# Strassen pairs of an output projection: one running weight sum instead of two, another product order, and other queues for the row stores

## The chip, the cores and the metric

One core of one Trainium2 chip runs the whole program. The metric is the device time of one execution in microseconds (us). Five engines work side by side and meet at semaphores: TensorE (PE), VectorE (DVE), ScalarE (ACT), GpSimd (POOL) and SyncE (SP, which here only issues transfers). ScalarE and GpSimd can issue transfers too.

## What is computed

Two encoder layers on 512 positions by 2048 features, in float32, then a last RMS norm. Each layer ends in a projection `mixed @ w_out` of 2048 by 2048 that is added to `x`; the next layer begins with the RMS norm of the result.

```python
def hybrid_layer(x, ...):
    h = rms_norm(x, norm_w)
    proj = jnp.einsum('bsd,de->bse', h, w_in)
    ...   # attention, short convolution and gated unit, each normed and gated
    mixed = jnp.concatenate([o_attn, o_conv, o_sgu], axis=-1)
    return x + jnp.einsum('bse,ed->bsd', mixed, w_out)

for layer in range(DEPTH):          # DEPTH = 2
    x = hybrid_layer(x, ...)
return rms_norm(x, final_norm_w)
```

## The kernel before, in words

Every float32 operand of a matmul is split into a high part (`wH`, a cast by ScalarE, line 98) and a remainder (`wL`, a subtraction by VectorE, line 99); three matmuls (high by high, low by high, high by low) make one product. `weight_parts` keeps five buffers of each part, so that the splits can run five weight tiles ahead of TensorE.

The input projection runs as 12 `product` calls per layer (line 201): eight weight pairs of 512 KB each, loaded by SP with `load_pair`, into four PSUM accumulators.

The output projection is the place of the change. `pair` (line 588) computes two column blocks `b0` and `b1` of 512 columns at a time by a scheme of Strassen and Winograd: rows are halved into two halves of 256 positions, the inner dimension into two halves of 1024, and seven products numbered 1 to 7 take the place of eight. One product is 8 inner tiles by 2 row tiles by 3 matmuls of 512 columns: 48 matmuls; a pair has 336, a layer two pairs, (0, 1) and (2, 3). The left operands (`A11`, `A12`, `A22` and the mixed sums `N1` to `N4`) are made by VectorE in `lower`, `mixed` and `upper`. The right operands are sums of four quarters of the weights, held in four tiles `X[i]` and four tiles `Y[i]` of 512 KB. In the order 1, 7, 3, 6, 5, 2, 4:

- `X` is loaded with the first quarter (line 591) and serves product 1. `Y` is loaded with the second quarter (line 593), and GpSimd issues an accumulating transfer that adds the third to it (line 594); it serves product 7. When product 1 has split `X[i]`, GpSimd issues an accumulating transfer of `Y[i]` onto `X[i]` (line 630), for product 6.
- Product 3 loads the third quarter afresh, and VectorE subtracts it from `X[i]` into `Y[i]` (line 632), for product 5.
- After product 6 has split `X[i]`, the fourth quarter is added by an accumulating transfer (line 634), for product 4. Product 2 loads the fourth quarter afresh.

Results go from PSUM to tiles `C[b, st]`: `begin` (line 576) copies by ScalarE and lets GpSimd issue an accumulating transfer of `x`; `gather` (line 582) adds further products by VectorE. A tile with all its products goes through `complete`. In layer 0 (line 710) that is: sum of squares by ScalarE, a store of the tile to DRAM issued by GpSimd (`x1d`, line 713), a transpose in blocks by VectorE (`Rows.put`, line 696), and after every second tile a store of 512 KB to `mv` issued by GpSimd (line 700). `arrive(b)` (line 718) loads `mv` back by SP (line 707) and scales it by ScalarE (line 725); that is the input of layer 1. In layer 1 (line 767) GpSimd multiplies some tiles with the last norm's weights (line 765), and `leave` scales and stores the rest.

Who works when: each engine takes its instructions in one fixed order, written when the kernel is built. Here the framework chooses that order by its own simulation of the program, so an engine's order is not that of the source; SP, ScalarE and GpSimd each hold their transfers in the same order as their other instructions. GpSimd is the only engine that issues accumulating transfers here.

Of the kernel before, what the change touches and what calls it, by code (L numbers as in the profile page):

```python
# [33 lines left out]
def trunk_kernel(ctx: ExitStack, tc: tile.TileContext, xT, xn, win, wout, wcols, convw, qkw, sgun,  # L34
# [224 lines left out]
    for l in range(L):  # L259
# [261 lines left out]
        def mixed(k, i):  # L521
            c, o = lo_of[k], hi_of[k]
            t, u = T(), T()
            nc.vector.tensor_tensor(out=u[:, :HALF], in0=c[:, :HALF], in1=c[:, HALF:], op=ALU.subtract)
            nc.vector.tensor_tensor(out=t[:, :HALF], in0=c[:, HALF:], in1=o[:, HALF:], op=ALU.subtract)
            nc.vector.tensor_tensor(out=t[:, HALF:], in0=t[:, :HALF], in1=c[:, :HALF], op=ALU.subtract)
            nc.vector.tensor_tensor(out=u[:, HALF:], in0=o[:, :HALF], in1=t[:, HALF:], op=ALU.add)
            for (a, b), src, g in (((N3, N4), u, free[2 * i]), ((N1, N2), t, free[2 * i + 1])):
# [40 lines left out]
        wy = [big.tile([P, 2, 2, S], F32, tag="kv", name=nm("wy"), bufs=2) for _ in range(2)]  # L569
        X = [wx[i // 2][:, i % 2] for i in range(4)]  # L570
        Y = [wy[i // 2][:, i % 2] for i in range(4)]
# [16 lines left out]
        def pair(b0, b1, C, complete, held, then={}):  # L588
            s0, s1 = wout[l, b0], wout[l, b1]
            for i in range(4):  # L590
                nc.sync.dma_start(out=X[i], in_=s0[i])
            for i in range(4):
                nc.sync.dma_start(out=Y[i], in_=s1[i])
                nc.gpsimd.dma_start(out=Y[i], in_=s1[4 + i], accum_op=ALU.add)
            c1 = [psum("sc") for _ in range(2)]
            c7 = [psum("acc") for _ in range(2)]
            for p in (1, 7, 3, 6, 5, 2, 4):
                if p == 1 or p == 6:
                    bank = c1
                elif p == 7 or p == 4:  # L600
                    bank = c7
                else:
                    bank = [psum("sc" if p == 2 else "acc") for _ in range(2)]
                A = operand[p]

                def matmuls(t, k, H, Lo):
                    ts = slice(t * P, (t + 1) * P)
                    a, c = A[k][0][:, ts], A[k][1][:, ts]
                    nc.tensor.matmul(bank[t], a, H, start=(k == 0 and p not in (6, 4)), stop=False, skip_group_check=True)  # L609
# [4 lines left out]
                for i in range(4):  # L614
# [4 lines left out]
                    else:  # L619
                        w = Y[i] if p in (7, 5) else X[i]  # L620
                    if held and p == 4:
                        for j in range(2):
                            H, Lo = [res.tile([P, S], F32R, tag=f"x{free[2 * (2 * i + j) + 1]}", name=nm("v"), bufs=2)
# [4 lines left out]
                    parts_i = [weight_parts(w[:, j]) for j in range(2)]  # L628
                    if p == 7:
                        nc.gpsimd.dma_start(out=X[i], in_=Y[i], accum_op=ALU.add)  # L630
                    elif p == 3:
                        nc.vector.tensor_tensor(out=Y[i], in0=X[i], in1=w, op=ALU.subtract)
                    elif p == 6:
                        nc.gpsimd.dma_start(out=X[i], in_=s0[4 + i], accum_op=ALU.add)
                    for j in range(2):
                        for t in range(2):
                            matmuls(t, 2 * i + j, *parts_i[j])
                for t in range(2):
# [6 lines left out]
                    elif p == 3:  # L645
                        begin(C, b1, t, bank[t], 1.0)
                    elif p == 6:
                        begin(C, b0, 2 + t, bank[t], 1.0)
                        gather(C, b1, t, bank[t], ALU.subtract)
                        gather(C, b1, 2 + t, bank[t], ALU.subtract)  # L650
                    elif p == 5:
                        gather(C, b1, t, bank[t], ALU.add)
                        gather(C, b1, 2 + t, bank[t], ALU.add)
                        if t == 1:
                            for st in range(ST):
                                complete(b1, st, bank[st % 2])
# [181 lines left out]
```

## Time and profile before

| what | value |
|---|---|
| median of 3 runs | 1497.47 us (1497.13 to 1497.98) |
| the profiled execution | 1496.9 us |
| its span, first to last instruction | 1494.9 us |
| TensorE busy | 1464.4 us, 98% |
| VectorE, ScalarE, GpSimd busy | 956.2, 680.8, 151.7 us |
| mean granted TensorE clock | 0.991 |
| moved by transfers | 241.64 MB |

The profiled execution stands 0.6 us under the median, and 2.0 us of it lie around the span. Busy shares are averages over a program with stages of different limits; a matmul counts as busy from its start to its modelled end, and consecutive ones overlap, so a stretch in which TensorE starts a matmul every 227 ns is as full as it gets.

### The profile page before, as it was taken

How to read it: one execution, taken by the hardware profiler on the slowest of the kernel's cores; microseconds unless marked ns; L12 is line 12 of the kernel's file. 1: busy time of each engine (PE TensorE's matmuls, PEld its weight loads, DVE VectorE, ACT ScalarE, POOL GpSimd, SP SyncE). 2: the span in 40 equal slices, each digit the busy share in tenths (PEclk: the TensorE clock that was granted, in tenths of full speed). 3: DMA queues.
4: the chain of work that ended last, by engine and by line, in shares of the span. 5: the costliest groups of instructions: out<-in, count | busy, mean ns of one | idle time of the engine just before them, and what ended most of it. 6: DMA issues, size and time to landing. Idle time of an engine off the chain costs nothing.

```text
span 1494.9 us, 18417 instructions
## 1 busy us (share of the span) xinstructions
PE 1464.4 (98%) x6422; PEld 1207.4 (81%) x6422; DVE 956.2 (64%) x1832; ACT 680.8 (46%) x1253; POOL 151.7 (10%) x166
## 2 busy tenths in 40 slices
PE   9999999999999999988989999999999999999997
PEld 7888888888888888866878888888888888888885
DVE  7657898645543467756746578986455534677666
ACT  7333365533332446536643343555333334465554
POOL 0110000000111001222200100000000110012232
PEclk9999999999999999999999999999999999999998
DMA  7334677633236634899863445776233376348975
GB/s 279 102 110 141 188 213 222 183 92 94 90 111 199 209 101 95 203 269 232 208 183 127 113 141 172 220 222 189 85 99 92 100 210 198 100 100 190 260 160 162
DMA packets 77117, 241.64 MB, mean 162 GB/s; under 512 B 9440, under 2 KB 10720, under 8 KB 74208
## 3 DMA queue, kind: packets, MB, share of 16 engines
q1 hardware_dynamic: 62784, 198.49, 42.6%
q0 software_dynamic: 13952, 41.95, 13.8%
q8 instruction: 50, 0.82, 0.2%
q14 instruction: 43, 0.35, 0.1%
q10 hardware_dynamic: 288, 0.03, 0.0%
HBM read 195.35 MB, written 36.70 MB: 155 GB/s over the span
## 4 chain that ended last, share of the span: by engine, by line
PE 91%; DMA 4%; issue 2%; POOL 1%; ACT 1%; DVE 1%; SPq 0%; POOLq 0%; ACTq 0%; DVEq 0%
PE acc L216 61%; PE sc L216 9%; PE acc L609 3%; PE acc L611 3%; PE acc L610 3%; PE sc L609 2%; PE sc L610 2%; PE sc L611 2%; PE sc L355 1%; PE ps L379 1%; PE sc L353 1%; PE ps L381 1%; PE sc L354 1%; PE ps L380 1%; DMA wx<-in_wout 1%
## 5 line engine op out<-in xcount | busy, mean ns | idle before, releaser
L99 DVE TENSOR_TENSOR wL<-wr,wH 128x512 fp32r<-128x512 f32 x448 | 304.1, 686 | 352.9 <-ACT wH L98 324.8
L98 ACT CAST wH<-wr 128x512 fp32r<-128x512 f32 x448 | 275.8, 621 | 522.6 <-PE acc L216 384.9
L216 PE MATMUL acc<-x,wH 128*128 128x512 f32 x1408 | 436.6, 389 | 0.0
L216 PE MATMUL acc<-wH,x 128*128 128x512 f32 x1280 | 393.1, 391 | 5.0 <-ACT wH L98 5.0
L216 PEld LDWEIGHTS acc<-x,wH 128*128 128x128 f32 x1408 | 264.2, 188 | 55.0
L216 PEld LDWEIGHTS acc<-wH,x 128*128 128x128 f32 x1280 | 240.5, 188 | 56.8 <-ACT wH L98 6.8
L216 PE MATMUL acc<-x,wL 128*128 128x512 f32 x704 | 273.2, 389 | 0.0
L216 PE MATMUL acc<-wL,x 128*128 128x512 f32 x640 | 244.6, 390 | 0.0
L216 PEld LDWEIGHTS acc<-x,wL 128*128 128x128 f32 x704 | 132.1, 188 | 27.4
L216 PEld LDWEIGHTS acc<-wL,x 128*128 128x128 f32 x640 | 120.3, 188 | 25.5 <-DVE wL L99 0.4
L99 DVE TENSOR_TENSOR wL<-wx,wH 128x512 fp32r<-128x512 f32 x88 | 60.2, 709 | 44.5 <-ACT wH L98 30.0
L105 POOL TENSOR_TENSOR s<-s,negh 128x4 f32<-128x4 f32 (+2 forms) x44 | 52.2, 1189 | 348.9 <-DVE s L103 343.5
L216 PE MATMUL sc<-wH,x 128*128 128x512 f32 x256 | 78.8, 389 | 0.0
L98 ACT CAST wH<-wx 128x512 fp32r<-128x512 f32 x88 | 52.7, 618 | 49.8 <-DMA wx<-in_wout 12.4
L609 PE MATMUL acc<-wH,n 128*128 128x512 f32 x192 | 74.7, 389 | 0.0
L610 PE MATMUL acc<-wH,n 128*128 128x512 f32 x192 | 74.7, 389 | 0.0
L362 ACT ACTIVATE p<-sc,sa 128x512 f32<-128x512 f32 x64 | 44.1, 689 | 61.4 <-DVE sa L359 43.3
L611 PE MATMUL acc<-wL,n 128*128 128x512 f32 x192 | 66.4, 391 | 1.1 <-DVE wL L99 0.9
L116 POOL TENSOR_TENSOR rc<-s,negh 128x4 f32<-128x4 f32 x5 | 5.1, 1013 | 514.3 <-DVE s L115 514.3
L216 PEld LDWEIGHTS sc<-wH,x 128*128 128x128 f32 x256 | 48.0, 188 | 10.0
L99 DVE TENSOR_TENSOR wL<-wy,wH 128x512 fp32r<-128x512 f32 x64 | 44.6, 720 | 9.7 <-ACT wH L98 6.7
L216 PE MATMUL sc<-wL,x 128*128 128x512 f32 x128 | 49.8, 389 | 0.0
(234 smaller groups left out, 2022.6 us busy)
## 6 DMA issues: line engine op xcount, KB each, us to landing
wr<-in_win SPq DMA_DIRECT2D x191, 512.0 KB, 3.6
rearr<-mv SPq DMA_DIRECT2D x104, 256.0 KB, 5.2
mv<-blk SPq DMA_DIRECT2D x22, 1024.0 KB, 4.8
wr<-in_wout SPq DMA_DIRECT2D x32, 512.0 KB, 4.8
wy<-in_wout SPq DMA_DIRECT2D x16, 512.0 KB, 6.8
wy<-in_wout POOLq DMA_DIRECT2D x16, 512.0 KB, 10.1
wx<-in_wout SPq DMA_DIRECT2D x16, 512.0 KB, 9.4
wx<-wy POOLq DMA_DIRECT2D x16, 512.0 KB, 5.2
```

Of the source, the lines that this page charges most:

```text
L98: nc.scalar.copy(H, src)
L99: nc.vector.tensor_tensor(out=Lo, in0=src, in1=f32(H), op=ALU.subtract)
L105: nc.gpsimd.tensor_tensor(out=r, in0=v, in1=negh[:, :n], op=ALU.pow)
L216: nc.tensor.matmul(acc[e], a, b, start=(kp == kps[0] and j == 0 and i == 0), stop=(kp == kps[-1] and j == 1 and i == 2))
L353: nc.tensor.matmul(sc, qH[:, ss], kH, start=True, stop=False)
L354: nc.tensor.matmul(sc, qH[:, ss], kL, start=False, stop=False)
L355: nc.tensor.matmul(sc, qL[:, ss], kH, start=False, stop=True)
L362: nc.scalar.activation(p, sc, AF.Exp, scale=SCALE, bias=nm_, accum_out=su)
L379: nc.tensor.matmul(po, a, pH[:, t], start=(t == 0), stop=False)
L609: nc.tensor.matmul(bank[t], a, H, start=(k == 0 and p not in (6, 4)), stop=False, skip_group_check=True)
L610: nc.tensor.matmul(bank[t], c, H, start=False, stop=False, skip_group_check=True)
L611: nc.tensor.matmul(bank[t], a, Lo, start=False, stop=(k == 7), skip_group_check=True)
```

## The change

In words: `Y` serves product 7 only and is taken from the pool anew in each pair. `X` grows three times by accumulating transfers straight from DRAM: the second quarter after product 1, the third after product 5, the fourth after product 6. The subtraction of line 632 and the transfer from `Y` to `X` are gone. The order is 1, 7, 5, 2, 6, 3, 4. Products 5 and 3 share two PSUM banks, and two of the twelve `gather` of a pair fall away. The operands in `mixed` are paired anew, `upper` is called after product 5. In layer 0 the `x1d` stores are issued by SP instead of GpSimd and the `mv` stores by ScalarE instead of GpSimd; `arrive` is called after products 5 and 2 of the second pair and, for blocks 3 and 2, inside the first product of layer 1, whose inner order changes. In layer 1 the last norm's weights are loaded after product 7, and GpSimd multiplies ten tiles instead of six.

```diff
-    def product(src, feature_major, before=None, kps=range(KT // 2)):
+    def product(src, feature_major, before=None, kps=range(KT // 2), then={}):
...
-        for kp in kps:
+        for n, kp in enumerate(kps):
+            if n in then:
+                then[n]()
...
-            acc = product(win[l, 0], False, kps=kps)
+            acc = product(win[l, 0], False, kps=kps, then=late)
...
-            for (a, b), src, g in (((N3, N4), u, free[2 * i]), ((N1, N2), t, free[2 * i + 1])):
+            for (a, b), src, g in (((N3, N1), t, free[2 * i]), ((N2, N4), u, free[2 * i + 1])):
...
+            wy = [big.tile([P, 2, 2, S], F32, tag="kv", name=nm("wy"), bufs=2) for _ in range(2)]
+            Y = [wy[i // 2][:, i % 2] for i in range(4)]
...
-            for p in (1, 7, 3, 6, 5, 2, 4):
...
+            c5 = [psum("acc") for _ in range(2)]
+            banks_of = {1: c1, 6: c1, 7: c7, 4: c7, 5: c5, 3: c5}
+            grow = {1: s1[:4], 5: s1[4:], 6: s0[4:]}
+            for p in (1, 7, 5, 2, 6, 3, 4):
+                bank = banks_of[p] if p in banks_of else [psum("sc"), psum("ps")]
...
-                        w = Y[i] if p in (7, 5) else X[i]
+                        w = Y[i] if p == 7 else X[i]
...
-                    parts_i = [weight_parts(w[:, j]) for j in range(2)]
-                    if p == 7:
-                        nc.gpsimd.dma_start(out=X[i], in_=Y[i], accum_op=ALU.add)
-                    elif p == 3:
-                        nc.vector.tensor_tensor(out=Y[i], in0=X[i], in1=w, op=ALU.subtract)
-                    elif p == 6:
-                        nc.gpsimd.dma_start(out=X[i], in_=s0[4 + i], accum_op=ALU.add)
+                    now = [weight_parts(w[:, j]) for j in range(2)]
+                    if p in grow:
+                        nc.gpsimd.dma_start(out=X[i], in_=grow[p][i], accum_op=ALU.add)
...
                     elif p == 5:
-                        gather(C, b1, t, bank[t], ALU.add)
                         gather(C, b1, 2 + t, bank[t], ALU.add)
...
+                    elif p == 6:
+                        begin(C, b0, 2 + t, bank[t], 1.0)
+                        begin(C, b1, t, bank[t], -1.0)
+                        gather(C, b1, 2 + t, bank[t], ALU.subtract)
+                        complete(b1, 2 + t, bank[t])
+                    elif p == 3:
+                        gather(C, b1, t, bank[t], ALU.add)
+                        complete(b1, t, bank[t])
...
-                        nc.gpsimd.dma_start(out=self.m[:, :, st - 1:st + 1],
+                        nc.scalar.dma_start(out=self.m[:, :, st - 1:st + 1],
...
-                nc.gpsimd.dma_start(out=x1d[b, st], in_=c)
+                nc.sync.dma_start(out=x1d[b, st], in_=c)
...
-            pair(2, 3, C, complete, False, {6: lambda: arrive(1), 5: lambda: arrive(0), 2: lambda: arrive(3)})
+            pair(2, 3, C, complete, False, {5: lambda: arrive(0), 2: lambda: arrive(1)})
...
-            arrive(2)
-            kps = (2, 3, 0, 1, 6, 7, 4, 5)
+            kps, late = (0, 1, 2, 3, 6, 7, 4, 5), {4: lambda: arrive(3), 6: lambda: arrive(2)}
...
+            for b in range(2):
+                for st in (0, 2, 1, 3):
+                    weighted(b, st)
...
-        pair(2, 3, C, complete, True, {3: weights_of_the_last_norm})
+        pair(2, 3, C, complete, True, {7: weights_of_the_last_norm})
```

## Rows read from the trace of the kernel before

**Rows 1.** Chain that ended last: start us, us, what; a steady stretch of layer 0.
```profile
52.66 87.07 PE acc L216 x384
```
**Rows 2.** Timeline of TensorE: start us, us, instruction, [idle before it <-releaser].
```profile
580.51 0.39 PE L609 MATMUL sc<-wH,a 128*128 128x512 f32 x1
...
645.14 0.50 PE L609 MATMUL acc<-wH,hA 128*128 128x512 f32 x1 [2.19 <-ACT wH L98]
...
663.50 1.21 PE L611 MATMUL acc<-wL,hA 128*128 128x512 f32 x2 [4.20 <-DVE wL L99]
...
678.48 0.79 PE L609 MATMUL sc<-wH,a 128*128 128x512 f32 x1 [5.84 <-ACT wH L98]
...
751.70 0.39 PE L611 MATMUL acc<-wL,hA 128*128 128x512 f32 x1
...
758.57 1.63 PE L216 MATMUL acc<-wH,x 128*128 128x512 f32 x4 [3.76 <-ACT wH L98]
...
1329.56 0.39 PE L609 MATMUL sc<-wH,a 128*128 128x512 f32 x1
...
1483.70 0.39 PE L611 MATMUL acc<-v,hA 128*128 128x512 f32 x1
```
**Rows 3.** Windows: stretch, its us, busy per engine, granted clock, DMA share, GB/s.
```profile
580.50:667.00 86.50, 80.11 (x337) 65.15 (x336) 64.14 (x105) 48.04 (x91) 22.04 (x28) 0.96 0.82 208
667.00:752.00 85.00, 79.16 (x338) 64.84 (x337) 55.82 (x86) 50.25 (x94) 20.60 (x28) 0.96 0.88 225
1329.50:1405.00 75.50, 75.50 (x333) 62.02 (x333) 57.57 (x94) 45.50 (x88) 15.77 (x18) 1.00 0.84 204
1405.00:1484.00 79.00, 77.94 (x342) 63.63 (x340) 58.70 (x85) 42.24 (x81) 26.25 (x24) 1.00 0.69 162
752.00:830.00 78.00, 74.24 (x321) 60.71 (x320) 40.42 (x91) 32.86 (x63) 5.96 (x8) 0.98 0.50 154
...
580.50:600.00 19.50, 19.50 (x87) 16.14 (x86) 19.50 (x36) 16.16 (x31) 3.52 (x4) 1.00 0.60 108
...
660.00:680.00 20.00, 10.66 (x36) 8.34 (x37) 8.77 (x14) 3.21 (x7) 5.46 (x8) 0.84 0.86 243
```
**Rows 4.** Timeline of GpSimd, its transfers: start us, us, issue, [idle before <-releaser].
```profile
461.08 1.06 POOL L594 DMA_DIRECT2D wy<-in_wout  x1 [1.33 <-PE sc L216]
...
470.60 0.91 POOL L594 DMA_DIRECT2D wy<-in_wout  x1 [4.72 <-issue]
...
631.28 0.89 POOL L594 DMA_DIRECT2D wy<-in_wout  x1 [8.03 <-DVE wL L99]
...
657.73 0.74 POOL L700 DMA_DIRECT2D mv<-blk  x1 [4.59 <-issue]
```
**Rows 5.** Transfers, window 461.0 to 461.25: issue, KB each, us to landing.
```profile
wy<-in_wout POOLq DMA_DIRECT2D x1, 512.0 KB, 9.3
```
**Rows 6.** Chain that ended last, around the waits: start us, us, what.
```profile
666.67 11.04 DMA wx<-in_wout
...
739.81 7.04 DMA mv<-blk
```
**Rows 7.** Timelines of VectorE and of SP's queue around 663 us.
```profile
661.57 1.30 DVE L696 STREAM_TRANSPOSE blk<-p 128x512 f32<-128x512 f32 x2 [8.13 <-DMA mv<-blk]
...
665.27 1.29 SPq L707 DMA_DIRECT2D rearr<-mv  x3
```
**Rows 8.** Queues in window 1328 to 1334, one accumulating transfer: packets, MB, share.
```profile
q0 software_dynamic: 144, 0.52, 46.2%
```
**Rows 9.** Queues, window 562.9 to 566.5: one plain load of 512 KB.
```profile
q1 hardware_dynamic: 144, 0.52, 47.8%
```
**Rows 10.** Lines 632, 152, 765: duration ns min/median/max, first and last start us.
```profile
L632 DVE TENSOR_TENSOR wy<-wx,wr x16: 1215/1222/1226, 594.4 to 1428.5; 128x1024 f32<-128x1024 f32 x16
L152 SPq DMA_DIRECT2D mv<-blk x24: 326/327/338, 70.6 to 1248.3; - x24
L765 POOL TENSOR_TENSOR c<-c,fr x5: 1279/1742/3067, 1443.1 to 1473.1; 128x512 f32<-128x512 f32 x5
```

More of the change, by code (lines that the diff above doesn't have):

```diff
@@ L523, in mixed @@
             t, u = T(), T()
[L524 to L527, printed above, removed]
-            for (a, b), src, g in (((N3, N4), u, free[2 * i]), ((N1, N2), t, free[2 * i + 1])):
+            nc.vector.tensor_tensor(out=t[:, :HALF], in0=c[:, :HALF], in1=c[:, HALF:], op=ALU.subtract)
+            nc.vector.tensor_tensor(out=t[:, HALF:], in0=c[:, HALF:], in1=o[:, HALF:], op=ALU.subtract)
+            nc.vector.tensor_tensor(out=u[:, :HALF], in0=t[:, HALF:], in1=c[:, :HALF], op=ALU.subtract)
+            nc.vector.tensor_tensor(out=u[:, HALF:], in0=o[:, :HALF], in1=u[:, :HALF], op=ALU.add)
+            for (a, b), src, g in (((N3, N1), t, free[2 * i]), ((N2, N4), u, free[2 * i + 1])):
                 h, lo = [res.tile([P, S], F32R, tag=f"x{g}", name=nm("n"), bufs=2) for _ in range(2)]
@@ L608, in matmuls @@
                     a, c = A[k][0][:, ts], A[k][1][:, ts]
-                    nc.tensor.matmul(bank[t], a, H, start=(k == 0 and p not in (6, 4)), stop=False, skip_group_check=True)
+                    nc.tensor.matmul(bank[t], a, H, start=(k == 0 and p not in (6, 3, 4)), stop=False,
+                                     skip_group_check=True)
                     nc.tensor.matmul(bank[t], c, H, start=False, stop=False, skip_group_check=True)
@@ L619, in pair @@
                     else:
-                        w = Y[i] if p in (7, 5) else X[i]
+                        w = Y[i] if p == 7 else X[i]
                     if held and p == 4:
                         for j in range(2):
-                            H, Lo = [res.tile([P, S], F32R, tag=f"x{free[2 * (2 * i + j) + 1]}", name=nm("v"), bufs=2)
+                            H, Lo = [res.tile([P, S], F32R, tag=f"x{free[2 * (2 * i + j)]}", name=nm("v"), bufs=2)
                                      for _ in range(2)]
@@ L627, in pair @@
                         continue
[L628 to L634 removed]
+                    now = [weight_parts(w[:, j]) for j in range(2)]
+                    if p in grow:
+                        nc.gpsimd.dma_start(out=X[i], in_=grow[p][i], accum_op=ALU.add)
                     for j in range(2):
                         for t in range(2):
[L637 removed]
+                            matmuls(t, 2 * i + j, *now[j])
                 for t in range(2):
@@ L749, in leave @@
                 o = C[b, st]
-                if st < 2 or b == 2:
+                if b == 2 or b == 3 and st < 2:
                     nc.vector.scalar_tensor_tensor(out=o, in0=o, scalar=r, in1=fr[b], op0=ALU.mult, op1=ALU.mult)
@@ L758, in weights_of_the_last_norm @@
         def weights_of_the_last_norm():
+            f = big.tile([P, 4, S], F32, tag="kv", name=nm("fr"), bufs=2)
             for b in range(4):
-                f = res.tile([P, S], F32, tag=f"x{free[2 * b]}", name=nm("fr"), bufs=2)
-                nc.sync.dma_start(out=f, in_=frow[b * S:(b + 1) * S].partition_broadcast(P))
-                fr.append(f)
+                nc.sync.dma_start(out=f[:, b], in_=frow[b * S:(b + 1) * S].partition_broadcast(P))
+                fr.append(f[:, b])
+            for b in range(2):
+                for st in (0, 2, 1, 3):
+                    weighted(b, st)
         def weighted(b, st):
@@ L768, in complete @@
             squares(b, st, junk)
-            if b == 3 and st == 3:
-                for bb, ss in ((0, 2), (1, 2), (3, 2), (0, 3), (1, 3), (3, 3)):
-                    weighted(bb, ss)
-            if b == 2:
+            if b == 3 and st > 1:
+                weighted(b, st)
+            if b == 2 and st > 1 or b == 3 and st < 2:
                 leave(st)
         C = tiles(0, 1, False)
-        pair(0, 1, C, complete, False, {7: upper})
+        pair(0, 1, C, complete, False, {5: upper})
         cs_ = [big.tile([P, 2, S], F32, tag="o", name=nm("c"), bufs=2) for _ in range(2)]
```

21 lines of the change are left out of this document (2 added, 19 removed).

## The prediction

> **What bounds the kernel now.** I read the engines first: TensorE is busy 98% of the span, so at most some tens of us can be won, and they must lie where TensorE waits. To find them I compare each stage with a steady stretch: 384 matmuls in 87.07 us, 0.2267 us each [rows 1]. The two pairs of layer 0 have 2 x 336 = 672 matmuls, 152.4 us at that pace. They run from 580.51 to 751.93 (the last start and one pace more), 171.4 us [rows 2]: 19.0 us are lost. The same 672 in layer 1 run from 1329.56 to 1483.93, 154.4 us: 2.0 lost. From 752 to 830, across the change of layers, 321 matmuls take 72.8 of 78 us [rows 3]: 5.2 lost. Together 26.2 us. Nothing else that the change touches delays TensorE, and the tail of 11 us after the last matmul keeps its form.
>
> The waits are four: 2.19, 4.20, 5.84 and 3.76 us [rows 2]. After each, TensorE also runs slowly for a while: the granted clock was 0.84 from 660 to 680, after two waits, and 0.96 over each pair of layer 0 against 1.00 in layer 1 [rows 3]; the level between 1.2 and 2.4 GHz falls after the idling, and that is why 19.0 exceeds the three waits of layer 0 (12.2) by 6.8.
>
> Then I ask why layer 0 and layer 1, with the same products in the same order, differ by 17 us. Layer 0 alone has the stores `x1d` and `mv`, both in GpSimd's order. GpSimd's issues show a limit: the fourth transfer onto `Y` went out at 470.60, after 4.72 us of idling that nothing visible ends [rows 4], and the first, issued at 461.08, had landed 9.3 us later, at 470.4 [rows 5]. So here GpSimd had three accumulating transfers of 512 KB on the way and no more. An `mv` store stands the same way: 4.59 us before the one at 657.73 [rows 4]. Its lateness is what TensorE feels. VectorE waited 8.13 us for an `mv` store to leave its buffer, with `wL` splits behind the transpose [rows 7]: the wait at 663.50. SP held loads for `arrive` ahead of two `X` loads, and a load issued at 666.67 took 11.04 us [rows 6, 7]: the wait at 678.48. At the change of layers an `mv` store of 7.04 us [rows 6] and its loads stand ahead of weight casts on ScalarE: the wait at 758.57. The wait at 645.14 is of another kind: GpSimd idled 8.03 us up to the prefetch of the next `Y` at 631.28 [rows 4], because `Y` is in use until product 5, and a `begin` stood behind it.
>
> **The change part by part.** *Queues.* Per pair of layer 0 GpSimd loses 8 `x1d` and 4 `mv` and gains 4 growths: 32 transfers become 24. ScalarE's own issue of `mv` has no row; the nearest is SP's, 0.327 us [rows 10], so 8 x 0.33 = 2.6 us on an engine busy 98.3 of 171.5 us [rows 3]: hidden, unless ScalarE waits at it for the transposes. That wait blocks the casts behind it, and VectorE's `wL` and TensorE after them; five split buffers, 5 x 6 matmuls = 6.8 us, cover it. Bounds: 0 to 10 us, I take 0. SP's `x1d` waits for the tile, with weight loads behind it; the same cover, the same price.
>
> *Y.* It is free after product 7, so its next load and accumulation can be done three products earlier. The wait at 645.14 goes.
>
> *X.* Each growth has two products, 21.8 us, from split to next use. Issue and landing took 9 to 12 us where transfers crowd [rows 5, 6], so about 8 us of lateness is absorbed. The order of growths and `begin` on GpSimd adds lateness, up to a few us.
>
> *VectorE.* It loses 8 subtractions of 1.22 us and 4 gathers per layer. It was busy 64 of 86.5 us [rows 3] and on no path except behind the transposes: worth nothing beyond what is counted.
>
> *Traffic.* This is the cost. Per pair 12 accumulating transfers of 512 KB become 16. Alone, one occupied the 16 transfer engines for 46.2% of 6 us, 2.77 us [rows 8]; a plain load 47.8% of 3.6 us, 1.72 us [rows 9]. So each layer gains 8 x 2.77 = 22.2 us of transfer work. Busy now: in layer 0 0.82 x 86.5 + 0.88 x 85 = 145.7 us, in layer 1 0.84 x 75.5 + 0.69 x 79 = 117.9 us [rows 3]. The new sums: 168 and 140 us. Layer 0's exceeds the 152.4 us of its matmuls. Not all is waited for: by the start of the last product (141.5 us) six `x1d` (0.86 each, half a plain load), two `mv`, four `arrive` loads and four weight loads of the next layer, 5.2 + 3.4 + 3.4 + 6.9 = 19 us, need not have landed, and block 3's four loads, 3 us, move out. So 146 us are due in 141.5, and the engines idle at first, for lack of work (share 0.60 in the first 19.5 us [rows 3]), some 10 us. Lateness: 146 + 10 - 141.5 = 15 us, of which 8 are absorbed: 7 us of waiting stay in layer 0. In layer 1: 140 less 7 for eight stores of the output, plus 10, is 143 against 141.5: absorbed.
>
> *Layer change.* `arrive(3)` and `arrive(2)` now stand inside the first product, whose first four weight pairs need only blocks 0 and 1, ready earlier. Of 5.2 us I leave 1.2 (bounds 0 and 5.2).
>
> *Layer 1's norm weights.* GpSimd does ten multiplications of 1.3 to 3.1 us [rows 10] instead of six, eight of them while it also issues growths: 8 x 1.7 = 14 us inside two products' time. Against that, 2.0 us of waits may go. I take no change (bounds: 2 won, 8 lost).
>
> *Weighed against a rule.* The trace has GpSimd idle at its issue until an earlier transfer landed [rows 4, 5]; by it the move is worth the waits at 663.50, 678.48 and 758.57. The Trainium skill, page "DMA: Bandwidth & Descriptors", section "Issuing engines are not separate DMA queues", says that transfers from all issuing engines run on the same 16 engines and that spreading them saves only sequencer time. By that rule 8 x 0.7 us of issue would be saved and all waits kept. The rows speak against it for `mv`, and for it in that the sum of traffic stays.
>
> **Sum.** Lost now 26.2; left 7 + 1.2 + 2 = 10.2; won 16.0. The profiled execution took 1496.9 us (2.0 of them around its span); 1496.9 - 16.0 = 1480.9, and the median of the runs stands 0.6 above it: 1481.5.
>
> **Rivals.**
> A, the forecast: 1481.5, own range 1475 to 1488. Chance 0.50.
> B, clean: transfers absorb each other and all waits of layer 0 and the layer change go, 24.2 us: 1473, down to 1470. For it: the first pair of layer 1 runs at a share of 0.84 without a wait [rows 3]. Against: the 168 us. Chance 0.15.
> C, the queue was not the cause: the 16 engines are, and each transfer lands as late as now. Of 26.2 nothing is won, small shifts either way: 1494.5 to 1500. For it: landings of 8 to 11 us in crowded stretches [rows 5, 6], whoever issues. The rule above gives this. Against: 657.73. Chance 0.13.
> D, slower: growths become the bound. It decides when less than 22.2 us of a layer's idle transfer time is usable. Idle are 171.5 - 145.7 = 25.8 us in layer 0 and 154.5 - 117.9 = 36.6 in layer 1. If half is usable, 22.2 - 12.9 = 9.3 and 22.2 - 18.3 = 3.9 us come on top and no wait is won: 1497.5 + 13.2 = 1510.7. For it: the idle time lies at the stages' ends, where nothing is ready. Against: stores need not be awaited. Chance 0.12.
> E, the change doesn't free what it frees on paper: the built order puts ScalarE or SP at a store before its data, with weight loads or casts behind. Price: 8 such stands of up to 3 us, half covered: 10 us of the 16 go back, 1491. Chance 0.10.
>
> **How the numbers follow.** A is likeliest: 1481.5. About 0.2%, 3 us, is what a measurement of this kernel can tell from no change. Faster: A, B, E, 0.75; same: most of C, 0.13; slower: D, 0.12. The range from 1470 to 1497 takes in B, A, E and half of C; outside lie D and the rest, below 2 in 10.
>
> **What would show it.** Right: no idle before GpSimd's issues longer than 3 us that only a landing ends; granted clock near 1.00 in both pairs of layer 0; transfer share above 0.9 there; pairs of layer 0 in about 160 us. Wrong by D: waits of TensorE on casts of `wx`, with growths landing after 12 us and more, in both layers. Wrong by C: the same waits at the same products. Wrong by E: idle ScalarE or SP before line 700 or 713.

## The result and the profile after

The changed kernel takes 1520.36 us (median of 4 runs, 1518.6 to 1521.26), the kernel before beside it 1497.3: a ratio of 1.0152, 95% interval 1.0134 to 1.0169. The forecast was 1481.5 and the range ended at 1497: the sign was wrong, and the time is that of no rival. D, the slower one, came nearest in kind and stood at 1510.7.

The profiled execution has a span of 1518.0 us against 1494.9. The page's engine and transfer totals after the change:

```profile
PE 1470.6 (97%) x6422; PEld 1211.0 (80%) x6422; DVE 936.2 (62%) x1806; ACT 681.3 (45%) x1255; POOL 155.6 (10%) x162
...
DMA packets 83517, 250.03 MB, mean 165 GB/s; under 512 B 9696, under 2 KB 15072, under 8 KB 80608
```

VectorE is relieved by 20 us and 8.4 MB more are moved, both as the diff says. TensorE's waits, from its timeline (start, duration, instruction, [idle before it <-releaser]), answer [rows 2]:

```profile
581.22 0.39 PE L609 MATMUL sc<-wH,a 128*128 128x512 f32 x1
...
624.23 0.79 PE L612 MATMUL sc<-wL,hA 128*128 128x512 f32 x1 [4.31 <-DVE wL L99]
...
665.21 1.22 PE L612 MATMUL acc<-wL,hA 128*128 128x512 f32 x2 [5.28 <-DVE wL L99]
...
697.62 0.80 PE L609 MATMUL acc<-wH,n 128*128 128x512 f32 x1 [6.22 <-ACT wH L98]
...
769.15 2.07 PE L218 MATMUL acc<-wH,x 128*128 128x512 f32 x4 [3.80 <-ACT wH L98]
...
1338.78 0.39 PE L609 MATMUL sc<-wH,a 128*128 128x512 f32 x1
...
1380.73 0.79 PE L612 MATMUL sc<-wL,hA 128*128 128x512 f32 x1 [3.26 <-DVE wL L99]
...
1464.95 0.50 PE L612 MATMUL sc<-wL,hA 128*128 128x512 f32 x1 [4.63 <-DVE wL L99]
...
1505.76 0.39 PE L612 MATMUL acc<-v,hA 128*128 128x512 f32 x1
```

Counted as in the prediction (672 matmuls of two pairs need 152.4 us), the two pairs of layer 0 now run from 581.22 to 759.75: 178.5 us, 26.1 lost where 19.0 were. Those of layer 1 run from 1338.78 to 1505.99: 167.2 us, 14.8 lost where 2.0 were. So 19.9 of the 23.1 us lie in the pairs; 1.4 came between the layers' pairs, 0.7 before them, 1.1 at the end. (Two shorter waits of layer 0, 1.15 us at 744.12 and 1.56 at 755.04, are not shown above.)

The windows answer [rows 3]; the columns are stretch, its us, busy time of PE, PEld, DVE, ACT, POOL, granted clock, DMA share, GB/s:

```profile
581.20:672.20 91.00, 81.41 (x338) 66.28 (x336) 58.30 (x99) 47.55 (x92) 20.03 (x23) 0.92 0.95 238
672.20:759.80 87.60, 78.68 (x338) 64.00 (x337) 51.30 (x82) 49.98 (x96) 16.55 (x19) 0.96 0.93 224
1338.80:1421.40 82.60, 79.34 (x337) 65.08 (x336) 55.17 (x93) 48.45 (x92) 20.09 (x23) 0.96 0.93 224
1421.40:1506.00 84.60, 78.99 (x337) 63.61 (x335) 51.82 (x73) 41.28 (x78) 33.85 (x31) 0.98 0.72 153
...
620.00:640.00 20.00, 15.77 (x59) 12.86 (x60) 12.18 (x20) 7.13 (x15) 5.51 (x7) 0.83 1.04 228
660.00:680.00 20.00, 14.79 (x55) 12.02 (x56) 12.85 (x21) 9.70 (x19) 3.48 (x4) 0.83 0.96 280
```

Share times stretch gives transfer work of 86.5 + 81.5 = 168 us in layer 0 and 76.8 + 60.9 = 138 us in layer 1. The prediction worked out 168 and 140. The sums were right; what they do to TensorE was not.

Four of the waits, 17.5 us together, end at `wL` on VectorE, and VectorE itself now waits long for `x` (who, line, released by: us in total, times, longest):

```profile
DVE c L584 <- DMA c<-x: 23.7, 7, 7.8
...
DVE c L584 <- DMA c<-in_xn: 17.3, 4, 8.0
```

In the kernel before, gathers waited for `x` 5.8 us in all. L584 is `gather`: VectorE adds a product's bank to an accumulator whose `x` is still on its way. The chain into the wait at 624 shows the order (start, duration, what):

```profile
600.04 6.37 DMA wy<-in_wout
...
610.49 0.86 POOL wy L596
...
612.96 0.86 POOL c L580
...
615.55 7.24 DMA c<-in_xn
...
622.88 0.06 DVE c L584
...
623.49 0.69 DVE wL L99
...
624.23 0.79 PE sc L612
```

Product 7 ended at about 603 (the pair's start and 96 paces); its `x` went out only behind the accumulations onto the next pair's `Y`, landed at 622.8, and the `wL` splits stood behind the gather on VectorE. The waits at 665.21, 1380.73 and 1464.95 stand behind such gathers in the same way. After each such wait the granted clock falls (0.83 in the two windows), and a matmul takes 0.43 us instead of 0.23, the lower of the two levels, 1.2 instead of 2.4 GHz: 11.1 us more after these four waits. Waits and slow matmuls make 28.6 us; against that the kernel before's waits at 645.14 and 663.50 are gone (663.50 stood behind an `mv` store [rows 7], the new one at 665.21 behind `x`).

The longest wait, at 697.62, is of another kind. ScalarE, whose casts TensorE wants, stands at the scaling in `arrive` (line 720 here) until the loads of `mv` have landed:

```profile
694.50 2.56 ACT L720 ACTIVATE t<-rearr,wc 128x512 f32<-128x512 f32 x4 [9.47 <-DMA rearr<-mv]
```

Layer 1 shows the waits on `x` best, since no store goes out in it before 1502. GpSimd's timeline in its first pair:

```profile
1351.88 1.79 POOL L580 DMA_DIRECT2D p<-x  x2 [4.69 <-ACT p L578]
1358.04 0.86 POOL L596 DMA_DIRECT2D wy<-in_wout  x1 [4.37 <-DVE wL L99]
1360.30 0.86 POOL L596 DMA_DIRECT2D wy<-in_wout  x1 [1.40 <-DMA wy<-in_wout]
1360.90 1.17 POOL L631 DMA_DIRECT2D wx<-in_wout  x1
1366.92 0.88 POOL L596 DMA_DIRECT2D wy<-in_wout  x1 [4.85 <-issue]
1369.41 0.86 POOL L580 DMA_DIRECT2D c<-x  x1 [1.61 <-ACT wH L98]
1371.93 0.86 POOL L580 DMA_DIRECT2D c<-x  x1 [1.67 <-issue]
```

and VectorE's:

```profile
1377.79 0.69 DVE L584 TENSOR_TENSOR c<-acc,c 128x512 f32<-128x512 f32 x1 [6.64 <-DMA c<-x]
1379.39 0.69 DVE L584 TENSOR_TENSOR c<-acc,c 128x512 f32<-128x512 f32 x1 [0.91 <-DMA c<-x]
1380.00 2.49 DVE L99 TENSOR_TENSOR wL<-wr,wH 128x512 fp32r<-128x512 f32 x4
```

The landing can be added up. From 1352.0 to the second gather's start at 1379.4 are 27.4 us, with the 16 engines at a share of 0.98: 26.9 us of work. In that time landed: four transfers of `x` of 256 KB (two named `p`), at half the price of [rows 8] (an estimate) 5.5 us; four plain loads of `Y`, 6.9 us at [rows 9]; three accumulations onto `Y`, 8.3; one growth of product 5, 2.8; two plain loads `wr`, 3.4. The sum is 26.9 us. That it meets the measured work so well is luck in part, as the two queues show (window 1352 to 1379: packets, MB, share of the 16 engines; q0 is GpSimd's, q1 SyncE's):

```profile
q0 software_dynamic: 1193, 3.31, 65.4%
q1 hardware_dynamic: 864, 3.15, 32.7%
```

By them GpSimd's transfers took 17.7 us, where the prices give 16.6 for those that landed (0.16 MB of theirs belongs to later ones), and SyncE's 8.8, where they give 10.3. What stands firm is that the engines were full in the stretch in which `x` was to be issued and to land. In the kernel before they were not; the same 27 us, from 13 us after the pair's start, and then the changed kernel's:

```profile
1342.70:1370.00 27.30, 27.30 (x121) 22.38 (x120) 23.57 (x36) 14.54 (x26) 6.23 (x8) 1.00 0.70 157
1352.00:1379.40 27.40, 25.47 (x113) 20.77 (x111) 16.45 (x28) 13.14 (x22) 8.63 (x10) 1.00 0.98 239
```

### The profile page after: what moved, and what is told of

It reads as the page before. It is cut to its first block, busy times and chain, and to the rows that moved or that the text cites. A ratio compares the mean times of both kernels' runs of the same rounds, so it can differ in the third digit from the quotient of the medians.

```text
span 1518.0 us, 18400 instructions
## 1 busy us (share of the span) xinstructions
PE 1470.6 (97%) x6422; PEld 1211.0 (80%) x6422; DVE 936.2 (62%) x1806; ACT 681.3 (45%) x1255; POOL 155.6 (10%) x162
## 4 chain that ended last, share of the span: by engine, by line
PE 85%; DMA 7%; issue 4%; POOL 2%; ACT 1%; DVE 1%; SPq 0%; POOLq 0%; ACTq 0%; DVEq 0%
PE acc L218 59%; PE sc L218 9%; PE sc L612 2%; PE sc L609 2%; PE sc L611 2%; DMA mv<-blk 2%; PE acc L609 2%; PE acc L612 2%; PE acc L611 2%; DMA rearr<-mv 1%; DMA c<-in_xn 1%; PE sc L357 1%; PE ps L381 1%; PE ps L383 1%; PE sc L355 1%
## 5 line engine op out<-in xcount | busy, mean ns | idle before, releaser
L218 PEld LDWEIGHTS acc<-wL,x 128*128 128x128 f32 x640 | 120.5, 188 | 25.5 <-DVE wL L99 0.4
L99 DVE TENSOR_TENSOR wL<-wx,wH 128x512 fp32r<-128x512 f32 x120 | 86.7, 745 | 35.2 <-ACT wH L98 25.8
L98 ACT CAST wH<-wx 128x512 fp32r<-128x512 f32 x120 | 72.5, 619 | 71.0 <-PE ps L611 25.4
L631 POOL DMA_DIRECT2D wx<-in_wout x48 | 42.1, 884 | 350.0 <-DVE wL L99 321.5
L609 PEld LDWEIGHTS acc<-wH,n 128*128 128x128 f32 x192 | 36.5, 190 | 17.2 <-ACT wH L98 9.7
```

The lines of the kernel that those rows point to most:

```text
L98: nc.scalar.copy(H, src)
L99: nc.vector.tensor_tensor(out=Lo, in0=src, in1=f32(H), op=ALU.subtract)
L218: nc.tensor.matmul(acc[e], a, b, start=(kp == kps[0] and j == 0 and i == 0), stop=(kp == kps[-1] and j == 1 and i == 2))
L631: nc.gpsimd.dma_start(out=X[i], in_=grow[p][i], accum_op=ALU.add)
```

## The experiments

Theory A: the waits come from where `x` is issued and how soon it is wanted. Theory B: they come from the transfers' volume. Each expectation stands in its own words. "Lost" is counted per layer's two pairs as above; the changed kernel has 26.1 and 14.8.

**No wait on x.** `begin`'s transfer goes to a spare place, so no gather waits for it.

```
-            nc.gpsimd.dma_start(out=c, in_=src, accum_op=ALU.add)
+            spare = dram.tile([P, S + 128], F32, tag="spare", name=nm("spare"), bufs=16)
+            nc.gpsimd.dma_start(out=spare[:, :S], in_=src, accum_op=ALU.add)
```

> The changed kernel, with the accumulating transfer of x in begin (line 580) sent to a spare tile in DRAM instead of C: as many transfers in the same queue, but no gather waits for one. Leaves out the addition of x. Theory A (the gather that follows begin by one product instead of two waits for a late x, and the remainder splits wait behind it on VectorE): the four waits of VectorE that end in TensorE's waits at 624, 665, 1381 and 1465 us, 17.5 us and 11 us of slow clock after them, go: about 1492 us, 1485 to 1500. Theory B (the 16 added transfers fill the transfer engines, whoever waits first): the waits move to the growths of X, and the time stays 1513 to 1522. Theory C (the stores by ScalarE and SP are the loss): 1515 to 1522, with the waits near 698 and 755 us grown.

1510.66 us (1.0090, 1.0075 to 1.0105), in no range that was expected. Layer 0 lost 13.7, layer 1 2.8. But layer 0's pairs began 16.7 us later than in the changed kernel, at 597.9: layer 0's transfers, now waiting for nothing, were issued within the first 42 us and delayed the first stage. Without that delay it would be about 1494, worked out and not run. In layer 0 the losses speak for the gathers' wait as the path by which the time reaches TensorE, since 12 transfers of this kind (layer 1's) still went out within its pairs. In layer 1 they don't separate the wait from the volume: all 16 of its transfers went out before 782 us. There the path is what the timelines above show.

**x loaded ahead.** SyncE loads `x` into the accumulators at the head of the pair (plain loads); `begin` becomes an operation of VectorE.

```
-            nc.scalar.activation(c, bank, AF.Copy, scale=sign)
-            nc.gpsimd.dma_start(out=c, in_=src, accum_op=ALU.add)
+            gather(C, b, st, bank, ALU.add if sign > 0 else ALU.subtract)
...
+            nc.sync.dma_start(out=C[b, st], in_=src)   # in pair(), for 8 (b, st)
```

> The changed kernel, with x loaded into each C by a plain load of SP ahead of its first product, and begin turned into an add or subtract by VectorE; the 16 accumulating transfers per layer become 16 plain loads. Same result as the reference. Theory A: 1480 to 1495, no wait of VectorE on a tile of x over 2 us. Theory B: 16 x (1.62 - 0.86) = 12 us of transfer work less per layer, so some 1505 to 1515. Theory C: 1512 to 1522.

1497.76 us (1.0004, 0.9995 to 1.0013), 2.8 us above theory A's range: all 22.6 us come back, and none of the forecast gain. Here too two things moved at once: `x` is issued early, and a plain load takes the engines less than an accumulating one [rows 8, 9]. Layer 1 lost 5.8, layer 0 still 21.6; no gather waits for `x`, and the longest wait left is again the one behind `arrive`:

```profile
696.88 0.79 PE L609 MATMUL acc<-wH,n 128*128 128x512 f32 x1 [7.29 <-ACT wH L98]
```

**Y held back.** Tiny reads after product 2 keep `Y` in use, so that its transfers come two products later.

```
+                        for q in wy:
+                            nc.vector.tensor_tensor(out=small(1), in0=bank[t][:, :1], in1=q[:, 0, 0, :1], op=ALU.add)
```

> The changed kernel, with Y kept in use until product 2 by four one-column reads by VectorE, so that the next pair's accumulations onto Y leave GpSimd's order ahead of product 7's begin. If theory A holds and the accumulations onto Y are what makes x late: the waits at 624 and 1381 us go (7.6 us and 6.4 us of slow clock), 1506 us, 1500 to 1512. If A holds and the growths alone make x late: 1515 to 1520 with both waits kept. Theory B: the waits move to the later products, 1515 to 1525. Theory C: no change.

1530.41 us (1.0217, 1.0202 to 1.0232), above every range. The waits at 624 and 1381 are gone, but others came (TensorE's timeline):

```profile
651.21 0.80 PE L609 MATMUL acc<-wH,n 128*128 128x512 f32 x1 [7.14 <-ACT wH L98]
...
675.15 0.79 PE L609 MATMUL sc<-wH,a 128*128 128x512 f32 x1 [7.22 <-ACT wH L98]
```

Lost 28.1 and 25.5. Moving the burst away from `x` doesn't pay for it.

**The queues alone.** In the kernel before, `mv` is stored by ScalarE and `x1d` by SyncE.

```
-                        nc.gpsimd.dma_start(out=self.m[:, :, st - 1:st + 1],
+                        nc.scalar.dma_start(out=self.m[:, :, st - 1:st + 1],
...
-                nc.gpsimd.dma_start(out=x1d[b, st], in_=c)
+                nc.sync.dma_start(out=x1d[b, st], in_=c)
```

> The kernel before, with nothing but the two queue moves: mv stores issued by ScalarE, x1d stores by SP. The prediction's step (GpSimd's order was the cause of three of layer 0's waits): 1478 to 1488. The rival that the 16 shared engines decide: 1494 to 1500, waits kept. Theory C (a store on ScalarE or SP lands later and holds up casts or loads): 1500 to 1510.

1497.33 us (0.9994, 0.9985 to 1.0004): nothing. Layer 0 lost 19.0 as before, and the worst wait is longer than any in [rows 2]:

```profile
679.79 0.79 PE L609 MATMUL sc<-wH,a 128*128 128x512 f32 x1 [9.38 <-ACT wH L98]
```

The first two `mv` stores took 16.2 and 19.7 us to land under ScalarE's issue, where 3.7 and 3.4 had been enough under GpSimd's. But they went out at 642.66 and 643.42 instead of 657.73 and 661.84, and so landed at 658.9 and 663.2 instead of 661.5 and 665.2: issued 15 and 18 us earlier, they landed 2.6 and 2.1 us earlier. The step *Queues* of the prediction falls here.

**A later gather.** The bank of product 7 is gathered after product 6; `begin` follows product 5. Except in the last pair, product 3's gather follows product 4 (not shown).

```
-                        begin(C, b1, 2 + t, bank[t], -1.0)       # after product 7
...
-                        gather(C, b1, 2 + t, bank[t], ALU.add)   # after product 5
+                        begin(C, b1, 2 + t, bank[t], 1.0)        # after product 5
...
+                        gather(C, b1, 2 + t, c7[t], ALU.subtract)   # after product 6
```

> The changed kernel with two steps between begin and gather again. C of block b1, lower rows, is begun after product 5 (from product 5's bank) and not after product 7; product 7's bank is subtracted after product 6, with product 6's. Except in the last pair, product 3's gather is put after product 4. As many transfers and operations as in the changed kernel, same result. Theory A (x lands too late for a gather one product after its begin): the waits at 624, 665, 1381 and 1465 us go, 28 us with the slow clock after them; layer 1's pairs lose about 3 us instead of 14.8, layer 0's about 12 to 18 instead of 26.1; 1490 to 1502 us. Theory B (the added transfers fill the engines): 1512 to 1522, both layers' losses kept at other products.

1530.33 us (1.0221, 1.0205 to 1.0236), above both ranges. It tests nothing cleanly: product 7's bank is ready long before, so the built order let VectorE stand at that gather early, for 11.87 us in layer 1's first pair. The same edit together with a larger descriptor space and later `arrive` calls:

> late_gather with the doubled space, and in layer 0 arrive(0) and arrive(1) called after products 6 and 3 of the second pair instead of 5 and 2, so that ScalarE's scaling of late rows stands behind more of the casts. Theory A: the wait near 697 us (7 us and 2 of slow clock) goes too, 1478 to 1492. Theory B: 1505 to 1520.

1527.64 us (1.0205, 1.0190 to 1.0220), above both ranges; VectorE stands at the same gather for 11.41 us.

**A later gather with a true dependence.** As above, but product 6's bank is gathered first, so that VectorE can't come to it before two products have run.

```
+                        begin(C, b1, 2 + t, bank[t], 1.0)            # after product 5
...
                         gather(C, b1, 2 + t, bank[t], ALU.subtract)  # product 6's bank, as it was
+                        gather(C, b1, 2 + t, c7[t], ALU.subtract)
```

> The changed kernel with one difference: for the quarter of product 7, ScalarE's copy and GpSimd's transfer of x are issued after product 5 as before, but the first gather onto them is that of product 6's bank, and that of product 7's bank follows it. So the transfer has two products (about 22 us of TensorE each, 12 sets of 16 matmuls) instead of one before VectorE needs it, as the kernel before gave it. Theory A (the second layer loses its 14.8 us because VectorE stands at a gather whose x was issued one product earlier, and the next weight sums queue behind it): the wait at 1381 us goes, the second layer's loss falls from 14.8 us to 3 to 6, the first layer's from 26 to about 19; 1495 to 1508, most likely 1501. Theory B (the transfers' own volume, eight accumulating transfers more of 512 KB in each pair of pairs, is what is paid): the loss moves to the next wait, 1513 to 1522.

1520.74 us (1.0155, 1.0140 to 1.0170): no change, in theory B's range. The wait at 1381 is gone, and at product 6's `x` another stands (timelines of VectorE and TensorE):

```profile
1412.02 0.69 DVE L584 TENSOR_TENSOR c<-acc,c 128x512 f32<-128x512 f32 x1 [6.95 <-DMA c<-x]
...
1417.24 0.79 PE L612 MATMUL acc<-wL,hA 128*128 128x512 f32 x1 [7.81 <-DVE wL L99]
```

Theory A, as far as it blamed one gather's place, falls: the wait only moved on to the next transfer of `x`.

**Without the third growth.** The four accumulating transfers after product 5 are left out (the sum misses that quarter); order and queues are those of the change.

```
-            grow = {1: s1[:4], 5: s1[4:], 6: s0[4:]}
+            grow = {1: s1[:4], 6: s0[4:]}
```

> The changed kernel without the four accumulating transfers that grow the running sum after product 5 (it leaves out the third quarter's rows of x's side of the sum, so the products that use them are computed from a smaller sum); everything else stands, so each layer has as many accumulating transfers in its pair stage as the kernel before, and order and queues are those of the change. Theory B (volume decides): the loss of the first layer falls to 15 to 20 us, the second's to 2 to 5; 1495 to 1505. Theory A (x is issued too late for its gather): those four are issued behind product 5, after the transfer of x that the late gather needs, so the waits at 624 and 1381 us stay at 3 to 5 us each; 1508 to 1518.

1498.31 us (1.0005, 0.9995 to 1.0014): 22 us back; lost 18.5 and 2.6, time and losses in theory B's ranges. The four transfers of 512 KB a pair that the change adds are its whole loss, and the new product order and queues alone, with the old volume, equal the kernel before. (The growth after product 1, which reads DRAM where the kernel before read `Y`, is in this kernel too, so that exchange isn't the loss.) Its engines are as full while `x` is on its way, only for 23.7 us instead of 27.4:

```profile
1344.60:1368.30 23.70, 23.70 (x106) 19.61 (x106) 16.61 (x28) 12.30 (x22) 6.99 (x8) 1.00 0.98 242
```

**Why they cost it.** The same four transfers as plain loads onto the same places, by GpSimd and by SyncE (the addition is left out):

```
+                        if p == 5:
+                            nc.gpsimd.dma_start(out=X[i], in_=grow[p][i])   # or nc.sync
```

> The changed kernel with the four transfers after product 5 as plain loads of the same rows onto the same places, issued by GpSimd where the accumulating ones were (it leaves out the addition of this quarter, so the products that follow use a smaller sum). A plain load takes 1.72 us of the 16 engines, an accumulating one 2.77. If the engines' time is what is paid: leaving the four out altogether gave 22 us back, plain loads give back 1.05/2.77 of it, 8 us: 1510 to 1515. If the place in GpSimd's order is what is paid: nearly as slow as the changed kernel, 1516 to 1521. If only the accumulating form costs: 1498 to 1503.

> The same four plain loads, issued by SyncE, so that nothing of GpSimd's order stands behind them (the same part is left out). If the engines' time is what is paid: as with GpSimd's, 1510 to 1515, and x's transfers land no earlier than there. If the place in GpSimd's order is what is paid: x is issued as early as with the four left out, and the time is 1498 to 1503. If only the accumulating form costs: 1498 to 1503 for both kernels of this pair, so the other one tells this from the order.

1505.1 us (1.0044, 1.0029 to 1.0059) by GpSimd, 1508.69 (1.0072, 1.0057 to 1.0087) by SyncE. Neither time lies in a range that was expected; the nearest were the accumulating form for the first (1498 to 1503) and the engines' time for the second (1510 to 1515). But for these loads GpSimd's order as the cause is out, since taking them out of it is slower. GpSimd's timeline in the SyncE kernel shows when `x` went out:

```profile
1362.06 0.89 POOL L596 DMA_DIRECT2D wy<-in_wout  x1 [2.84 <-DVE wL L99]
1364.82 0.88 POOL L580 DMA_DIRECT2D c<-x  x1 [1.87 <-ACT wH L98]
1368.61 0.86 POOL L580 DMA_DIRECT2D c<-x  x1 [2.92 <-issue]
```

and one moment's transfers in it (issue, KB each, us to landing):

```profile
wy<-in_wout POOLq DMA_DIRECT2D x1, 512.0 KB, 10.1
wx<-in_wout SPq DMA_DIRECT2D x1, 512.0 KB, 14.8
```

No growth stands ahead of `x` in that order, yet its two transfers took 9.9 and 8.7 us to land, against 6.1 and 6.2 in the kernel without the third growth. Then two and three of the four:

```
+                    if p in grow and (p != 5 or i < 2):   # or 3
```

> The changed kernel with two of the four accumulating transfers after product 5 (the other two places of the running sum miss this quarter). They take 2 x 2.77 = 5.5 us of the 16 engines in each of the four pairs. Theory in step: each transfer costs the same, half of the 22 us is paid: about 1509. Theory of a slack: with four, 11.1 us per pair go in and 22/4 = 5.5 us are paid, so some 5.6 us per pair find room; two find room whole: 1498 to 1501.

> The same with three of the four: 8.3 us of the 16 engines per pair. Theory in step: three quarters of the 22 us are paid: about 1515. Theory of a slack of 5.6 us per pair: 4 x (8.3 - 5.6) = 11 us are paid: about 1509.

1512.35 us (1.0096, 1.0075 to 1.0118) and 1512.46 (1.0097, 1.0082 to 1.0112). Neither in step (1509, 1515) nor a slack (1498 to 1501, 1509). Nor do the engines' prices order these kernels: two accumulating transfers a pair (5.5 us) cost 14 us, four plain loads (6.9 us) 7 and 10, and four accumulating ones (11.1 us) 22. So the accumulating form seems to cost more than its share of the 16 engines (surely beside the plain loads by GpSimd; beside those by SyncE the intervals overlap); in which way, no run here tells. One wait, that of layer 1's first pair, does follow a simple number in all of them: when the second gather on `x` starts after the pair began, and how long TensorE then waits at its next `wL` (from the two timelines of each kernel).

| kernel | pair began, us | second gather | difference | TensorE's wait |
|---|---|---|---|---|
| without the third growth | 1331.51 | 1368.26 | 36.75 | none |
| plain, by GpSimd | 1330.38 | 1369.68 | 39.30 | 1.95 |
| changed kernel | 1338.78 | 1379.39 | 40.61 | 3.26 |
| three of four | 1334.19 | 1374.84 | 40.65 | 3.29 |
| two of four | 1333.58 | 1374.51 | 40.93 | 3.58 |
| larger space (below) | 1336.39 | 1377.62 | 41.23 | 3.88 |
| stores by GpSimd (below) | 1344.17 | 1385.60 | 41.43 | 4.07 |
| plain, by SyncE | 1335.73 | 1377.42 | 41.69 | 4.33 |

In each row with a wait, difference minus wait is 37.35 or 37.36 us: the order of instructions is the same in all of them, so each us that `x` lands after that point is a us of TensorE. This is one wait of 2 to 4 us and not the whole time: plain loads by SyncE wait longest here and are yet among the faster kernels. In the first row VectorE waited for TensorE, not for `x`:

```profile
1368.26 0.69 DVE L584 TENSOR_TENSOR c<-acc,c 128x512 f32<-128x512 f32 x1 [1.79 <-PE ps L611]
```

With two, three or four growths one stands ahead of `x` in GpSimd's order, which is why their differences are alike. How the rest of the loss, outside this wait, divides among the growths stays open.

**Stores back to GpSimd** in the changed kernel (the edit of the queues, reversed):

> The changed kernel with its mv stores and x1d stores issued by GpSimd again, as in the kernel before. If the landing of transfers sets when the stores' tiles come free, whoever issues, this moves little: 1517 to 1524, as the same edit alone on the kernel before moved nothing (1497.3). If GpSimd's order, now with four growths more to issue, is what fills: slower, 1525 to 1535. If the mv stores' landings of 15 to 17 us under ScalarE's issue cost the first layer its wait at 697 us: faster, 1510 to 1516.

1522.67 us (1.0159, 1.0142 to 1.0176), as expected of the landings, and not to be told from the changed kernel by the intervals.

**Twice the space for GpSimd's descriptors**, in the changed kernel and in the kernel before:

```
-dynamic_dma_scratch_size=1024
+dynamic_dma_scratch_size=2048
```

> The changed kernel with the scratch space for GpSimd's transfer descriptors doubled, 2048 for 1024; every engine's order is the same. If GpSimd's issue limit (three accumulating transfers on the way) makes x late: the idle time before GpSimd's issues goes, x lands some 3 to 5 us earlier, 1500 to 1512. If the 16 transfer engines make it late (theory B): issues come earlier and landings take longer by as much, 1516 to 1523.

> The kernel before with the same doubled space. The prediction's step (GpSimd waits at its issues for landings, and that makes mv and x1d late): 1482 to 1490, the waits near 663 and 758 us gone. The engines decide: 1494 to 1500, the same waits.

1517.82 us (1.0135, 1.0119 to 1.0150) and 1491.33 (0.9962, 0.9947 to 0.9976), the first as theory B has it, the second between its two ranges. The limit on GpSimd's issues that [rows 4, 5] show was worth 6 us to the kernel before (layer 0 lost 14.0 instead of 19.0), and 2.5 by the medians to the changed one, whose intervals overlap. The trace of the changed kernel with the larger space tells whether that limit makes `x` late: GpSimd's issue of `x`, its two transfers (KB each, median us to landing), and VectorE's second gather:

```profile
1362.54 2.12 POOL L580 DMA_DIRECT2D c<-x  x2
...
c<-x POOLq DMA_DIRECT2D x2, 256.0 KB, 14.0
...
1377.62 0.69 DVE L584 TENSOR_TENSOR c<-acc,c 128x512 f32<-128x512 f32 x1 [0.55 <-DMA c<-x]
```

Counted from the pair's start, `x` went out at 26.1 and 26.8 us instead of 30.6 and 33.2, and landed at 39.9 and 41.1 instead of 38.9 and 40.5. Issued 4 to 6 us earlier, it landed no earlier: the limit on issues is not what makes it late.

**x loaded ahead and the larger space together**, on the kernel before and on the changed one:

> The kernel before, with x loaded into the accumulators by SyncE ahead of the pair and added to by VectorE (plain loads of 512 KB, 1.72 us of the 16 engines instead of the 2.77 of an accumulating transfer, and no wait of a gather on a transfer issued late), and with twice the space for GpSimd's descriptors. Theory A and B both expect it faster than the kernel before: the larger space alone gave 1491.3; eight transfers a layer at 1.05 us less give up to 8.4 us more in the first layer, which is short of transfers, and nothing in the second. 1480 to 1492. If VectorE's eight further operations of 512 columns a pair stood in the way, it would be above 1491.

> The changed kernel with x loaded into the accumulators ahead by SyncE (as in x_first, 1497.8) and with twice the space for GpSimd's descriptors. If GpSimd's issues, which stand until an earlier transfer has landed, still cost the changed kernel something once no gather waits on x, it gains the 6 us that the kernel before gained: about 1492. If the 16 engines alone are the bound there, as 1517.8 against 1520.4 for the changed kernel itself suggests, 1495 to 1498.

1491.89 us (0.9955, 0.9939 to 0.9972) and 1499.31 (1.0001, 0.9991 to 1.0011). The first lies in its range but not below the larger space alone, so loading `x` ahead gives the kernel before nothing beyond the space; the second lies above both of its ranges. The best version is the kernel before with the larger space, 1491.3 us (1491.9 with `x` ahead as well is not to be told from it); the best one built on the changed kernel that computes the whole sum is 1497.8.

## Why the prediction was wrong, step by step

Two steps failed. The waits that were to go with the new queues, `Y` and the layer change, 23.0 us in the sum before 7 were set against them, gave nothing back (the one at 645.14 went, others came): without the four growths, but with everything else of the change, the time was 1498.31. And the term for the growths, *Traffic*, was 7 us and measured 22. Together they are 38 of the 38.9 us by which the forecast missed.

*Traffic*: against the kernel without the four growths (18.5 and 2.6 lost), they cost 7.6 us in layer 0, where the step left 7, and 12.2 in layer 1, where "143 against 141.5: absorbed" left nothing. The 7 in layer 0 is luck, not mechanism. The step weighed a whole layer's transfers against a whole layer's matmuls, with one deadline at the last product, and took 8 us as absorbed once; the waits came in mid-pair, at gathers on `x`. The work is due in bursts. In layer 1's first pair 27 us of it, `x` included, had to land before the second gather, at a share of 0.98 where the kernel before had 0.70, while the pair's first 13 us (0.69) and the next pair (0.72) had room. The price was read from a transfer of `Y` onto `X` [rows 8]. A growth from DRAM that ran alone took 57.4% of 5.3 us, 3.04 us instead of 2.77 (window 1337.9 to 1343.2, GpSimd's queue):

```profile
q0 software_dynamic: 144, 0.52, 57.4%
```

*Y*: the wait at 645.14 did go, as forecast. But loads and accumulations onto `Y` three products earlier, 6.9 us and 8.3 of the 27 at these prices, now stand ahead of `x`. The prediction counted the wait won and not what the moved transfers are moved past.

*What was never priced*: `begin` to `gather`. The new order wants product 7's `x` after one product instead of two, and a late `x` holds VectorE, its `wL` splits and TensorE. It isn't the distance alone: the kernel before also has a one-product distance (product 3 to 6), and the later gather with a true dependence won nothing.

*Queues*: failed, and most of the forecast gain with it. The idle before GpSimd's issues was real [rows 4, 5], but moving the stores to other issuers gave 1497.33 us on the kernel before. Here the weighed rule was right: the Trainium skill, page "DMA: Bandwidth & Descriptors", section "Issuing engines are not separate DMA queues", says that spreading over issuers saves only sequencer time. The run agrees; its time lies in rival C's range. What the idle was worth shows under the larger descriptor space, 6 us. Even the small term was off: an `mv` issue by ScalarE took 0.52 us, not 0.327 (duration in ns, minimum, median, maximum, over the kernel):

```profile
L695 ACTq DMA_DIRECT2D mv<-blk x8: 520/521/587, 637.4 to 768.6; - x8
```

*VectorE* at nothing: not contradicted; the kernel without the third growth has the same relief and is no faster than the kernel before. *Layer change*, from 5.2 to 1.2: failed; a wait of 3.80 stands at 769.15 where 3.76 stood at 758.57 [rows 2], again with ScalarE at the scaling in `arrive`, and the stretch between the layers' pairs grew by 1.4 us. *Norm weights* at nothing: not contradicted, since layer 1 lost only 2.6 us without the third growth, with the same multiplications on GpSimd.

*Rival D* named the bound and was priced at 13.2 us, by taking half of the idle transfer time as usable. Its sign to look for was wrong: it expected waits on casts of `wx` with landings over 12 us. The growths landed in 8.5 us (median of 23 in layer 0; 10 to 12 between 623 and 652), and it was `x`, behind them, that was wanted first. Its chance of 0.12 looks low in hindsight: most of the won waits of the forecast rested on transfers that would land earlier while 22 us more of them a layer were added to engines already at 0.82 to 0.88 in layer 0 [rows 3].

## What to carry to other kernels

When a change adds transfers, add them up burst by burst against the next thing that waits for one, not over a stage; with the engines full, a transfer delays what is issued behind it. Replacing the arithmetic of an engine with time to spare, on data that is already on the chip (here a subtraction on VectorE), by transfers was no gain here, where the transfer engines were the fuller resource. Of a transfer that an earlier release sets free, ask what it now stands ahead of.

## What was not expected of the hardware

Accumulating transfers under GpSimd's issue went out only as earlier ones landed, and doubling the descriptor space took 6 us off the kernel before; with the engines full it took little off the changed one, whose `x` went out 4 to 6 us earlier and landed no earlier. `mv` stores, 4.0 us to landing by GpSimd (median), took 16.2 and 19.7 us by ScalarE for the first two in the kernel before, and yet landed 2 us earlier than there: they had only been issued 15 and 18 us sooner. Two accumulating transfers a pair cost 14 us, four plain loads by GpSimd 7, though the two should take the 16 engines less (5.5 against 6.9 us a pair); that stays unexplained.
